# Low parts of the first phase's weights: VectorE in place of GpSimd

## The chip, the cores and the metric

The kernel runs on one core of one Trainium2 chip. The metric is the device time of one execution in microseconds (us). The core has five engines that each work through a queue of their own in order: TensorE (PE: matmuls; its weight loads have rows of their own, PEld), VectorE (DVE), ScalarE (ACT), GpSimd (POOL) and SyncE (SP, which issues most DMAs).

## The reference

One layer of a decoder trunk on 512 tokens, model width 2048, everything in fp32:

```python
mod = silu(c) @ w_ada + b_ada                       # 3 x 2048
shift, scale, gate = split(mod, 3)
u = rms_norm(x, norm_w) * (1 + scale) + shift       # 512 x 2048
proj = u @ w_in                                     # 512 x 23552
# three token mixers on slices of proj (differential attention,
# retention, dilated windows), each times silu of its gate slice
y_b = (mixer_b * silu(z_b)) @ P_b                   # three times
m = sum(sigmoid(g_b) * y_b)
out = rms_norm(x + gate * (m @ w_out), final_norm_w)
```

This case concerns the beginning: the modulation (scale and shift), u, and the first nine blocks of 128 columns of `w_in` that are multiplied with it, columns of the merge gate g_c.

## The kernel before

**Matmuls in two parts.** An fp32 operand a is split into a high part h = fp32r(a) and a low part l = a - h. A product is then three matmuls: high x high, high x low, low x high. ScalarE makes the high parts by a copy that rounds, and another engine makes the low parts by a subtraction of two SBUF tensors. A weight tile comes by DMA into `wr`; its high part is `wh`, its low part `wl`. For u they are `uh` and `ul`, 16 tiles each (one for each 128 rows of the model width). `wr`, `wh` and `wl` have three buffers each, so a load into `wr` waits until both parts of the tile three loads earlier have been made.

**The modulation by VectorE.** silu(c) @ w_ada is a product with one row, so it isn't done as a matmul: `mod_sum` multiplies tiles of `w_ada` (1 MB parts, `wa` and `wb`) by columns of silu(c) and adds them up in `acc`, one row block after another: 8 scalar_tensor_tensor instructions on 128x256 in a part, or 4 on 128x512. `mod_cols` then lets TensorE sum `acc` over the partitions (8 matmuls with a vector of `ones`), and VectorE adds bias and norm weight: the columns `s` (named `s1` in the code) for scale, `sh` for shift. There are 32 parts: 2 of 128 columns, 14 of 256 columns (two for each group of columns), 16 of 512 (four for each group).

**The stages around the change**, in order of time:

1. Start (to 32 us): x is loaded, normalized by VectorE and transposed by TensorE, and ScalarE copies the transposes to `xT`.
2. Phase 0 (32 to 127 us): 16 steps, one for each 128 rows k of the width. Step k multiplies seven column blocks of `w_in` with xT[k] times scale (`scaled(k)`: ScalarE makes `uh`, VectorE `ul`): 7 matmuls uh·wh, 7 ul·wh, 7 uh·wl, into seven PSUM banks. The shift isn't known yet, so its share is added later. In each step VectorE also sums one part of the modulation. Every second step `mod_cols` gives the scale of two further tiles.
3. Middle (127 to 154 us): the seven banks are copied out (`spill`), and two more column blocks are done as two halves of 8 x 3 matmuls each (`w_half`, 128x1024 weights). Four more parts of the modulation are summed.
4. Phase 1 (154 to 240 us): 16 steps as in phase 0 on the last seven column blocks of `w_in`, now with the whole u = xT·s + sh (`uf` by VectorE, then `uh`, `ul`); `uf` is also written to DRAM and has two buffers. The shift comes in four groups of four tiles.

After 240 us the rest of the layer follows, with weights whose low parts VectorE makes.

**Who makes the low parts.** In `split_first` (lines 267 to 270) GpSimd makes those of both phases' 32 steps. In the middle, `w_half` (line 172) is called with `low=nc.gpsimd` for the first of the two column blocks, and with VectorE for the second. All other calls of `w_half` use VectorE.

**What sets the order.** The order on each engine is not only that of the code: a scheduler places instructions by its own estimates, apart from places pinned by hand (`tc.issue_after` holds `scaled(k)` behind the ScalarE part of `split_first`, and the sum of a part behind `ul`). So a moved instruction also changes the order of its neighbours. Engines wait for one another by semaphores, and whatever stands behind a waiting instruction on its engine waits too.

Of the kernel before, what the change touches and what calls it, by code (L numbers as in the profile page):

```python
# [10 lines left out]
F32 = mybir.dt.float32  # L11
# [54 lines left out]
def hybrid_kernel(ctx, tc, x, c, w_in, w_pa, w_pb, w_pc, w_out, w_ada, b_ada, norm_w, lam,  # L66
                  da_w, ret_w, fin_w, k_ident, k_causal, k_band, k_tri4, k_sel, k_cos, k_sin,
                  k_decay, out):
    nc = tc.nc
# [18 lines left out]
    act, dve, pe, sync, pool = (Ordered(e) for e in (nc.scalar, nc.vector, nc.tensor, nc.sync, nc.gpsimd))  # L88
# [11 lines left out]
    def pj():  # L100
        return psum.tile([P, 512], F32, tag="pj", name="pj", bufs=2)

    def at():
        return psum.tile([P, 512], F32, tag="at", name="at", bufs=6)

    NF, NM = 7, 2
    w_in = w_in[0]
# [45 lines left out]
    def w_load(src, k0, c0):  # L153
        r, h, l = w_tiles([P, 8, P])
        sync.dma_start(out=r, in_=src[k0:k0 + 1024, c0:c0 + P].rearrange("(j p) c -> p j c", p=P))
        return r, h, l

    def w_half(src, k0, c0, rot=False, tiles=None, low=dve):

        if tiles is not None and len(tiles) == 2:  # L160
            return tiles
        r, h, l = tiles or w_load(src, k0, c0)
        if rot:
            for a in range(2):
                for e in range(2):
                    o = a * 64 + e * 32
                    rv = r[:, :, a * 64:a * 64 + 64].rearrange("p j (d e) -> p j e d", e=2)[:, :, e, :]
                    act.copy(h[:, :, o:o + 32], rv)
                    dve.tensor_sub(l[:, :, o:o + 32], rv, h[:, :, o:o + 32].bitcast(F32))
        else:  # L170
            act.copy(h, r)
            low.tensor_sub(l, r, h.bitcast(F32))  # L172
        return h, l

    def mm3(ps, ah, al, bh, bl, start, stop):
        pe.matmul(ps, lhsT=ah, rhs=bh, start=start, stop=False)
        pe.matmul(ps, lhsT=ah, rhs=bl, start=False, stop=False)
        pe.matmul(ps, lhsT=al, rhs=bh, start=False, stop=stop)
# [81 lines left out]
    def load_first(i):  # L260
        phase, k = steps[i]
        g0 = G_C + (0 if phase == 0 else NF + NM) * P
        r, h, l = w_tiles([P, NF, P])
        sync.dma_start(out=r, in_=w_in[k * P:(k + 1) * P, g0:g0 + NF * P].rearrange("p (b c) -> p b c", c=P))
        firsts[i] = (r, h, l)

    def split_first(i):
        r, h, l = firsts[i]
        halves[i] = act.copy(h, r).ins
        nc.gpsimd.tensor_sub(l, r, h.bitcast(F32))  # L270

    wb = [None]
    mod_load()
# [39 lines left out]
    def mod_cols(m):  # L313
        half, c0, cw = MODS[m]
        acc = accs.pop(m)
        pc = pj()
        nch = cw // P
        chains = min(2, 512 // cw)
        for ci in range(nch):
            for a in range(chains):  # L320
                pe.matmul(pc[:, ci:ci + 1], lhsT=acc[:, a, ci * P:(ci + 1) * P], rhs=ones[:, 0:1],
                                 start=a == 0, stop=a == chains - 1)
        mod_finish(m, pc)
# [14 lines left out]
    def mod_step(n=1):  # L338
        for _ in range(n):
            if to_sum:  # L340
                m, part = to_sum.pop(0)
                mod_sum(m, part)
                mod_load()
# [33 lines left out]
    def scaled(k):  # L377
        act.activation(out=uh[k], in_=xT[:, k, :], func=AF.Copy, scale=s1[:, k:k + 1])
        return dve.scalar_tensor_tensor(out=ul[k], in0=xT[:, k, :], scalar=s1[:, k:k + 1],
                                        in1=uh[k].bitcast(F32), op0=ALU.mult, op1=ALU.subtract).ins  # L380

    for k in range(KC):
        tp = tps[k] if k < 6 else at()
        for i in range(3 if k < 6 else 0, NT):
            x_tr(tp, i, k)
        act.copy(xT[:, k, :], tp)
        if k == 0:
            scaled(0)
            split_first(0)
            m, part = to_sum.pop(0)  # L390
            mod_sum(m, part)
            mod_cols(m)
        if k == 4:
            split_first(1)
# [4 lines left out]
    def spill(ps, db, on_act):  # L399
        raw = wbp.tile([P, S], F32, tag="raw", name="raw", bufs=2)  # L400
        if on_act:
            act.copy(raw, ps)
        else:
            dve.tensor_copy(raw, ps)
        nc.scalar.dma_start(out=graw_dram[db], in_=raw)

    mids = []
    group_of = {(1 - half) * KC + c0 // P: m for m, (half, c0, cw) in enumerate(MODS) if m > 1}
    for i, (phase, k) in enumerate(steps):
        if k == 0:  # L410
            ps = [at() for _ in range(6)] + [pj()]
        if i + 2 < KC or KC <= i < 2 * KC - 2:
            load_first(i + 2)
        elif phase == 0:
            mids.append(w_load(w_in, (i + 2 - KC) * 1024, G_C + NF * P))
        if phase == 0 and k > 0:
            with tc.issue_after(halves[i]):
                low_part = scaled(k)
        elif phase == 1:
            uf = wbp.tile([P, S], F32, tag="uf", name="uf", bufs=2)  # L420
            dve.tensor_scalar(out=uf, in0=xT[:, k, :], scalar1=s1[:, k:k + 1], scalar2=sh[:, k:k + 1],
                              op0=ALU.mult, op1=ALU.add)
            act.copy(uh[k], uf)
            dve.tensor_sub(ul[k], uf, uh[k].bitcast(F32))
            nc.scalar.dma_start(out=u_dram[k], in_=uf)
        if i in (KC, KC + 1):
            split_first(i)
        if i + 1 < 2 * KC and i + 1 not in (1, KC, KC + 1):
            split_first(i + 1)
        r, h, l = firsts.pop(i)  # L430
        for b in range(NF):
            pe.matmul(ps[b], lhsT=h[:, b, :], rhs=uh[k], start=k == 0, stop=False)
        if i + 1 < 2 * KC and i + 1 != KC and (i + 1) in group_of:
            mod_cols(group_of[i + 1])
        for b in range(NF):
            pe.matmul(ps[b], lhsT=h[:, b, :], rhs=ul[k], start=False, stop=False)
        for b in range(NF):
            pe.matmul(ps[b], lhsT=l[:, b, :], rhs=uh[k], start=False, stop=k == KC - 1)
        if phase == 0 and k > 0:
            with tc.issue_after(low_part):  # L440
                mod_step()
        else:
            mod_step(2 if i == 0 else 1)
        if k == KC - 1 and phase == 0:
            for b in range(NF):
                spill(ps[b], b, b % 2 == 0)
            if phase == 0:
                mids.append(w_load(w_in, 0, G_C + (NF + 1) * P))
                for b in range(NM):
                    pb = pj() if b == 0 else at()  # L450
                    for half in range(2):
                        h, l = w_half(w_in, 0, 0, tiles=mids.pop(0), low=nc.gpsimd if b == 0 else dve)
                        if b == 0 and half == 0:
                            mids.append(w_load(w_in, 1024, G_C + (NF + 1) * P))
                        elif (b, half) != (1, 1):
                            load_first(KC + b)
                        for j in range(8):
                            kk = half * 8 + j
                            if kk == 10 and b == 1:
                                mod_cols(group_of[KC])  # L460
                            mm3(pb, h[:, j, :], l[:, j, :], uh[kk], ul[kk], kk == 0, kk == KC - 1)
                        mod_step()
                    spill(pb, NF + b, True)
# [278 lines left out]
    def cut():  # L742
        if loads:
            tiles, rot = loads.pop(0)
            entry.append(w_half(None, 0, 0, rot, tiles))

    def step(*extra):

        feed()
        for f in extra:  # L750
            f()
        cut()
        due, late[:] = list(late), []
        for f in due:
            f()
        return entry.pop(0)
# [44 lines left out]
    for n in range(LAST):  # L801
        c0, cw = GROUPS[n]
# [337 lines left out]
    for hd in range(8):  # L1140
        h, prev = heads[hd], heads[hd - 1] if hd else None
# [545 lines left out]
    for n in range(LAST):  # L1687
# [3 lines left out]
        for t, k in enumerate(range(0, KC, nk)):  # L1691
# [17 lines left out]
            h, l = step()  # L1709
# [12 lines left out]
    c0, cw = GROUPS[LAST]  # L1722
    for f in waiting:
        f()
    for i in range(NT):
# [14 lines left out]
        h, cs = hx[i][3], slice(512 - cw, 512)  # L1740
# [31 lines left out]
```

## Time and profile before

| | |
|---|---|
| median of 3 runs | 2590.24 us (2589.38 to 2594.89) |
| profiled execution, own time | 2591.96 us |
| span of its trace | 2590.2 us |
| VectorE busy, whole span | 1924.0 us (74%) |
| GpSimd busy, whole span | 263.7 us (10%) |
| ScalarE busy, whole span | 1134.5 us (44%) |
| the 34 subtractions by GpSimd | 20.7 to 232.5 us |
| granted TensorE clock, mean of the span | 0.995 |

The views used: the **page** (busy time of each engine); the **windows** (busy time of each engine, instructions, granted clock and DMA share between two times); the **groups** (instructions of one line, engine, operation and shape: count | busy time, mean duration in ns | idle time before them and what ended it); the **waits** (who waited for whom: total, times, longest); the **timeline** (start, duration, engine, line, operation, count of merged instructions, and in brackets the idle time before with what ended it). Helpers record most operations, so nearly all rows have line L86; the tile names tell them apart. A tile name stands as out<-in: `wl<-wr,wh` is the subtraction in question. DVE durations in a row run from start to end of one instruction; consecutive ones overlap by some 0.07 us, so a merged row of n instructions is a little shorter than n durations.

### The profile page before, as it was taken

How to read it: one execution, taken by the hardware profiler on the slowest of the kernel's cores; microseconds unless marked ns; L12 is line 12 of the kernel's file. 1: busy time of each engine (PE TensorE's matmuls, PEld its weight loads, DVE VectorE, ACT ScalarE, POOL GpSimd, SP SyncE). 2: the span in 40 equal slices, each digit the busy share in tenths (PEclk: the TensorE clock that was granted, in tenths of full speed). 3: DMA queues.
4: the chain of work that ended last, by engine and by line, in shares of the span. 5: the costliest groups of instructions: out<-in, count | busy, mean ns of one | idle time of the engine just before them, and what ended most of it. 6: DMA issues, size and time to landing. Idle time of an engine off the chain costs nothing. (4 is left out here: it accounts for less than half of the span.)

```text
span 2590.2 us, 36747 instructions
## 1 busy us (share of the span) xinstructions
PE 2519.2 (97%) x14539; PEld 2222.9 (86%) x14539; DVE 1924.0 (74%) x2682; ACT 1134.5 (44%) x1476; POOL 263.7 (10%) x327
## 2 busy tenths in 40 slices
PE   6999999999999999999999999999999999999998
PEld 5777777999999999999888888888888888777888
DVE  7994788778877888778787777447877657776554
ACT  4233433443443333333345666346666436653223
POOL 3332000000000000000000000210000120003100
PEclk9999999999999999999999999999999999999999
DMA  9776755656666666666566555564343573348543
GB/s 345 262 277 214 268 209 207 221 194 221 236 233 212 223 214 238 233 217 225 206 211 199 147 148 147 179 188 130 91 122 114 165 239 97 107 126 286 196 132 114
DMA packets 363953, 504.83 MB, mean 195 GB/s; under 512 B 18850, under 2 KB 237748, under 8 KB 363396
## 3 DMA queue, kind: packets, MB, share of 16 engines
q1 hardware_dynamic: 329732, 401.89, 47.5%
q0 software_dynamic: 27136, 92.13, 10.4%
q10 hardware_dynamic: 6912, 8.46, 0.9%
q8 instruction: 114, 1.87, 0.3%
q14 instruction: 59, 0.48, 0.1%
HBM read 450.37 MB, written 52.04 MB: 194 GB/s over the span
## 5 line engine op out<-in xcount | busy, mean ns | idle before, releaser
L86 ACT CAST xh<-xr 128x2048 fp32r<-128x2048 f32 x196 | 374.4, 1910 | 589.1 <-PE at L86 471.0
L86 DVE TENSOR_TENSOR xl<-xr,xh 128x2048 fp32r<-128x2048 f32 x196 | 449.1, 2291 | 184.5 <-ACT xh L86 183.3
L86 PE MATMUL pj<-uh,wh 128*128 128x512 f32 x944 | 372.5, 395 | 0.0
L86 PE MATMUL pj<-uh,wl 128*128 128x512 f32 x944 | 369.4, 391 | 2.6 <-POOL wl L172 2.6
L86 PE MATMUL pj<-ul,wh 128*128 128x512 f32 x944 | 369.1, 391 | 0.0
L86 DVE TENSOR_TENSOR wl<-wr,wh 128x1024 fp32r<-128x1024 f32 (+2 forms) x241 | 238.2, 1007 | 174.8 <-ACT wh L86 173.8
L86 ACT CAST wh<-wr 128x1024 fp32r<-128x1024 f32 (+2 forms) x275 | 239.1, 889 | 285.5 <-PE at L86 136.2
L86 DVE TENSOR_TENSOR xr<-xr 128x512 f32<-128x512 f32 x448 | 309.2, 690 | 15.0 <-DMA xr<-in_w_in_dram 3.3
L86 PE MATMUL at<-fh,xl 128*128 128x256 f32 x864 | 245.0, 284 | 1.9 <-DVE xl L86 1.9
L86 PE MATMUL at<-fh,xh 128*128 128x256 f32 x864 | 244.5, 283 | 0.0
L86 PE MATMUL at<-fl,xh 128*128 128x256 f32 x864 | 244.5, 283 | 0.0
L86 PEld LDWEIGHTS pj<-uh,wl 128*128 128x128 f32 x944 | 178.0, 189 | 40.8 <-POOL wl L172 3.0
L86 PEld LDWEIGHTS pj<-uh,wh 128*128 128x128 f32 x944 | 178.4, 189 | 35.6
L86 PEld LDWEIGHTS pj<-ul,wh 128*128 128x128 f32 x944 | 178.2, 189 | 35.6
L86 PEld LDWEIGHTS at<-fh,xl 128*128 128x128 f32 x864 | 165.5, 192 | 2.3 <-DVE xl L86 2.3
L86 PEld LDWEIGHTS at<-fh,xh 128*128 128x128 f32 x864 | 165.5, 192 | 0.0
L86 PEld LDWEIGHTS at<-fl,xh 128*128 128x128 f32 x864 | 165.5, 192 | 0.0
L86 PE MATMUL at<-ul,xh 128*128 128x256 f32 x576 | 163.0, 283 | 0.0
L86 PE MATMUL at<-uh,xh 128*128 128x256 f32 x576 | 163.0, 283 | 0.0
L86 PE MATMUL at<-uh,xl 128*128 128x256 f32 x576 | 163.0, 283 | 0.0
L86 PE MATMUL at<-yh,wh 128*128 128x512 f32 x288 | 112.5, 390 | 2.1 <-ACT wh L86 2.1
L86 PE MATMUL at<-yh,wl 128*128 128x512 f32 x288 | 112.2, 390 | 0.5 <-DVE wl L86 0.5
(389 smaller groups left out, 5724.1 us busy)
## 6 DMA issues: line engine op xcount, KB each, us to landing
xr<-in_w_in_dram SPq DMA_DIRECT2D x224, 512.0 KB, 4.4
xr<-in_w_in_dram SPq DMA_DIRECT2D x84, 1024.0 KB, 4.8
wr<-in_w_in_dram SPq DMA_DIRECT2D x116, 512.0 KB, 4.0
wa<-in_w_ada_dram SPq DMA_DIRECT2D x20, 1024.0 KB, 8.5
wr<-in_w_out_dram SPq DMA_DIRECT2D x32, 512.0 KB, 3.9
wr<-in_w_in_dram SPq DMA_DIRECT2D x32, 448.0 KB, 8.5
wb<-in_w_ada_dram SPq DMA_DIRECT2D x12, 1024.0 KB
bw<-in_w_in_dram SPq DMA_DIRECT2D x24, 384.0 KB, 5.6
```

What stands on the lines that cost most here:

```text
L86: return lambda *a, **k: pin(f(*a, **k))
```

## The change

Both calls on GpSimd become calls on VectorE: the 32 subtractions of `split_first` (128x896, one for each step of both phases) and the two of the first column block in the middle (128x1024). The parameter `low` of `w_half`, no longer needed, goes.

```diff
-    def w_half(src, k0, c0, rot=False, tiles=None, low=dve):
+    def w_half(src, k0, c0, rot=False, tiles=None):
...
             act.copy(h, r)
-            low.tensor_sub(l, r, h.bitcast(F32))
+            dve.tensor_sub(l, r, h.bitcast(F32))
...
     def split_first(i):
         r, h, l = firsts[i]
         halves[i] = act.copy(h, r).ins
-        nc.gpsimd.tensor_sub(l, r, h.bitcast(F32))
+        dve.tensor_sub(l, r, h.bitcast(F32))
...
-                        h, l = w_half(w_in, 0, 0, tiles=mids.pop(0), low=nc.gpsimd if b == 0 else dve)
+                        h, l = w_half(w_in, 0, 0, tiles=mids.pop(0))
```

Data, tiles, buffers, DMAs and SyncE's order stay the same. GpSimd keeps nothing to do before its first DMA after phase 1, and the two instructions that configure it stand before its first tensor operation, now in the attention stage at 1407 us. The places where VectorE's order changes, in three pieces.

VectorE at the start, where the fourth tile of x is normalized. `ss` is the sum of squares, `rstd` the reciprocal root (ScalarE takes the root between these two), `x_157` the tile of x, `acc` the sum of a part, `ul_122` the first `ul`; + is new, - is gone:

```order
 L86 TENSOR_TENSOR ss<-ss 128x1
+L86 TENSOR_TENSOR wl<-wr,wh 128x896
 L86 RECIPROCAL rstd<-rstd 128x1
 L86 TENSOR_SCALAR x_157<-x_157,rstd 128x1024 x2
 L86 TENSOR_SCALAR acc<-wa,sc 128x128 x2
-L86 SCALAR_TENSOR_TENSOR acc<-wa,sc,acc 128x128 x2
+L86 SCALAR_TENSOR_TENSOR acc<-wa,sc,acc 128x128 x4
 L86 SCALAR_TENSOR_TENSOR ul_122<-xT,s_99,uh_106 128x512
```

The first step's `wl` now stands between the sum of squares and the reciprocal.

VectorE in phase 0, two steps, first before and then of the change. `ul_127` to `ul_129` are the `ul` of steps 5 to 7; `s_99` are the scale columns, which wait for the matmuls with `ones`:

```order
L86 SCALAR_TENSOR_TENSOR ul_127<-xT,s_99,uh_111 128x512
L86 TENSOR_SCALAR acc<-wb,sc 128x256 x2
L86 SCALAR_TENSOR_TENSOR acc<-wb,sc,acc 128x256 x3
L86 TENSOR_TENSOR s_99<-pj,cols 128x2
L86 SCALAR_TENSOR_TENSOR acc<-wb,sc,acc 128x256
L86 SCALAR_TENSOR_TENSOR s_99<-s_99,cols 128x2
L86 SCALAR_TENSOR_TENSOR acc<-wb,sc,acc 128x256 x2
L86 SCALAR_TENSOR_TENSOR ul_128<-xT,s_99,uh_112 128x512
L86 SCALAR_TENSOR_TENSOR acc<-wa,sc,acc 128x256 x8
L86 SCALAR_TENSOR_TENSOR ul_129<-xT,s_99,uh_113 128x512
```

```order
L86 SCALAR_TENSOR_TENSOR ul_127<-xT,s_99,uh_111 128x512
L86 TENSOR_SCALAR acc<-wb,sc 128x256 x2
L86 SCALAR_TENSOR_TENSOR acc<-wb,sc,acc 128x256
L86 TENSOR_TENSOR s_99<-pj,cols 128x2
L86 SCALAR_TENSOR_TENSOR acc<-wb,sc,acc 128x256
L86 SCALAR_TENSOR_TENSOR s_99<-s_99,cols 128x2
L86 SCALAR_TENSOR_TENSOR acc<-wb,sc,acc 128x256 x4
L86 TENSOR_TENSOR wl<-wr,wh 128x896
L86 SCALAR_TENSOR_TENSOR ul_128<-xT,s_99,uh_112 128x512
L86 SCALAR_TENSOR_TENSOR acc<-wa,sc,acc 128x256 x7
L86 TENSOR_TENSOR wl<-wr,wh 128x896
L86 SCALAR_TENSOR_TENSOR acc<-wa,sc,acc 128x256
```

In each step one `wl` now stands shortly before that step's `ul`, and the scale columns come two instructions earlier. The next row of the second list is `ul_129`.

VectorE in phase 1, from the `ul` of step 2 to the second group of shift columns; `sh` are these columns, `uf` is the new u:

```order
 L86 TENSOR_TENSOR ul_124<-uf,uh_108 128x512
+L86 TENSOR_TENSOR wl<-wr,wh 128x896
+L86 SCALAR_TENSOR_TENSOR acc<-wa,sc,acc 128x512
+L86 TENSOR_TENSOR ul_125<-uf,uh_109 128x512
 L86 SCALAR_TENSOR_TENSOR acc<-wa,sc,acc 128x512 x2
-L86 TENSOR_TENSOR ul_125<-uf,uh_109 128x512
+L86 TENSOR_TENSOR wl<-wr,wh 128x896
 L86 SCALAR_TENSOR_TENSOR acc<-wa,sc,acc 128x512 x5
+L86 TENSOR_TENSOR wl<-wr,wh 128x896
 L86 SCALAR_TENSOR_TENSOR acc<-wb,sc,acc 128x512 x4
 L86 TENSOR_TENSOR sh<-pj,cols 128x4
 L86 TENSOR_SCALAR acc<-wb,sc 128x512
```

Three subtractions now stand ahead of the shift columns, among the same sums. On TensorE the order of the steps stays; only the `ones` matmuls at the end of the start stage come four transposes earlier.

## The prediction

> **What bounds the kernel now.** First the page, then the windows of the three stages that the change touches (columns: time, length, busy time and instructions of PE, PEld, DVE, ACT, POOL, granted clock, DMA share, GB/s):
>
> ```profile
> PE 2519.2 (97%) x14539; PEld 2222.9 (86%) x14539; DVE 1924.0 (74%) x2682; ACT 1134.5 (44%) x1476; POOL 263.7 (10%) x327
> ...
> 31.00:126.60 95.60, 87.35 (x406) 70.03 (x405) 90.58 (x156) 27.00 (x38) 39.58 (x16) 1.00 0.88 300
> 126.60:153.60 27.00, 24.43 (x105) 19.96 (x104) 24.37 (x32) 8.23 (x11) 8.26 (x3) 0.94 0.80 285
> 153.60:239.70 86.10, 81.99 (x361) 67.44 (x361) 56.48 (x68) 25.50 (x34) 31.79 (x14) 0.96 0.63 222
> ```
>
> Over the whole span TensorE sets the time. Not so here: in phase 0 VectorE is busy for 90.6 of 95.6 us, more than TensorE's 87.3, and in the other two stages the granted clock is below 1. The waits of TensorE in the three stages, in this order, name who is late:
>
> ```profile
> PE at L86 <- DVE ul L86: 3.5, 2, 1.9
> PE pj L86 <- DVE acc L86: 2.8, 4, 0.7
> PE at L86 <- ACT uh L86: 2.0, 4, 0.9
> ...
> PE pj L86 <- POOL wl L172: 2.6, 1, 2.6
> ...
> PE at L86 <- ACT uh L86: 4.1, 2, 3.7
> ```
>
> `ul` and `acc` are VectorE's, and `uh` waits for scale or `uf`, VectorE's too. So the question is what VectorE's queue gains or loses. The timeline at the beginning of phase 0 shows what GpSimd does to it:
>
> ```profile
> 29.03 4.07 POOL L270 TENSOR_TENSOR wl<-wr,wh 128x896 fp32r<-128x896 f32 x1 [5.96 <-ACT wh L86]
> 31.36 2.02 DVE L86 SCALAR_TENSOR_TENSOR acc<-wa,sc,acc 128x256 f32<-128x256 f32 x1
> ...
> 38.61 3.95 POOL L270 TENSOR_TENSOR wl<-wr,wh 128x896 fp32r<-128x896 f32 x1 [5.51 <-ACT wh L86]
> 40.57 2.27 DVE L86 SCALAR_TENSOR_TENSOR acc<-wa,sc,acc 128x256 f32<-128x256 f32 x1
> ```
>
> One `acc` on 128x256, begun while GpSimd subtracts, takes over 2 us and ends 0.28 us after GpSimd's end (33.38 after 33.10, 42.84 after 42.56). It stands still until GpSimd is done.
>
> **What the change takes from VectorE's queue, and adds.** Groups: GpSimd's 32 subtractions; the sums in phase 0; the same shapes where no GpSimd subtraction runs; then the nearest relatives of the new instruction, `wl` on 128x1024 and `ul` on 128x512, both by VectorE from two SBUF tensors:
>
> ```profile
> L270 POOL TENSOR_TENSOR wl<-wr,wh 128x896 fp32r<-128x896 f32 x32 | 77.2, 2420 | 138.1 <-ACT wh L86 129.0 <-PE pj L86 9.1
> ...
> L86 DVE SCALAR_TENSOR_TENSOR acc<-wa,sc,acc 128x256 f32<-128x256 f32 x56 | 34.0, 667 | 0.0
> L86 DVE SCALAR_TENSOR_TENSOR acc<-wb,sc,acc 128x256 f32<-128x256 f32 x42 | 28.4, 741 | 0.0
> L86 DVE SCALAR_TENSOR_TENSOR acc<-wa,sc,acc 128x512 f32<-128x512 f32 x11 | 12.0, 1092 | 0.2
> ...
> L86 DVE SCALAR_TENSOR_TENSOR acc<-wa,sc,acc 128x256 f32<-128x256 f32 x11 | 4.4, 472 | 0.0
> ...
> L86 DVE SCALAR_TENSOR_TENSOR acc<-wa,sc,acc 128x512 f32<-128x512 f32 x2 | 1.5, 748 | 0.0
> ...
> L86 DVE TENSOR_TENSOR wl<-wr,wh 128x1024 fp32r<-128x1024 f32 x2 | 2.4, 1219 | 0.0
> ...
> L86 DVE TENSOR_TENSOR ul<-uf,uh 128x512 fp32r<-128x512 f32 x2 | 1.4, 678 | 0.0
> ```
>
> Lost in phase 0 by standing still: 56 x (667 - 472) + 42 x (741 - 472) + 11 x (1092 - 748) ns = 10.9 + 11.3 + 3.8 = **26.0 us**. Added: 512 columns more cost 1219 - 678 = 541 ns, so 128x896 takes 1219 - 135 = 1084 ns, some 1.02 us of the queue since neighbours overlap (an estimate from these two rows). Phase 0 gets 14 of them and one of 128x1024: **15.5 us**. So VectorE gives away 26.0 and takes 15.5, and its busy time there falls from 90.6 to about 80.1 us. The gain is the standing still, not GpSimd's own time.
>
> One page of the Trainium skill speaks against the change: Perfetto Trace Analysis, section Optimizing Scalar/DVE Operations, says that when VectorE is saturated, handing work to ScalarE or even GpSimd can pay; it adds that the two share a port of SBUF, so that moving work between them might not help. The first half would keep GpSimd's share where it is; the rows above go with the second half, 26.0 us lost against 15.5 us of work.
>
> **Start, -1.3 us.**
>
> ```profile
> 19.70 0.93 ACT L86 CAST wh<-wr 128x896 fp32r<-128x896 f32 x1
> ...
> 21.05 2.03 DVE L86 TENSOR_TENSOR ss<-ss 128x1 f32<-128x1 f32 x1
> 23.12 0.29 ACT L86 ACTIVATE rstd<-ss,eps 128x1 f32<-128x1 f32 x1 [2.49 <-DVE ss L86]
> ```
>
> An addition of one column, `ss`, takes 2.03 us, because it too stands behind GpSimd's first subtraction. Without that it ends at about 21.15. The new `wl`, whose `wh` is ready at 20.63, fills VectorE to 22.2, while ScalarE takes the root; then the normalization goes on, at 22.3 in place of some 23.6 (23.12 + 0.29 and the reciprocal). The fourth tile's transposes and the copies behind them follow. Bounds: 0 to 1.9.
>
> **Phase 0, -9.5 us.** The first matmul, and one pair of steps on TensorE:
>
> ```profile
> 32.15 0.48 PE L86 MATMUL at<-uh,wh 128*128 128x512 f32 x1
> ...
> 98.03 1.13 PE L86 MATMUL pj<-ones,acc 128*128 128x1 f32 x8 [0.75 <-DVE acc L86]
> 99.03 1.63 PE L86 MATMUL at<-ul,wh 128*128 128x512 f32 x6
> ...
> 106.27 1.52 PE L86 MATMUL at<-uh,wl 128*128 128x512 f32 x6
> ...
> 107.86 1.52 PE L86 MATMUL at<-uh,wh 128*128 128x512 f32 x6
> ...
> 110.32 1.13 PE L86 MATMUL pj<-ones,acc 128*128 128x1 f32 x8 [0.72 <-DVE acc L86]
> ```
>
> The pair lasts 12.3 us. Seven matmuls need 1.59 us (106.27 to 107.86), a step of 21 thus 4.77, the `ones` 1.0: without waits the pair would last 10.5. Sixteen steps and seven groups of `ones` make 83.3 us; phase 0 now lasts 94.5 (32.15 to 126.6, where the middle's first matmul stands). So at most 11.2 us can go. VectorE alone would allow 10.5 (90.6 to 80.1, with the same 5 us of idle time). Both limits come out nearly alike, so I look at the order in a pair. After the scale columns VectorE does four sums (1.6 us), `wl` (1.0) and `ul` (0.7), so `ul` is there 3.5 us after the `ones`; TensorE wants it 4.8 us after (three blocks of seven). Both steps of the pair come out with 1 to 2 us to spare, and the sums are complete well ahead of the next `ones`. I leave out 1 us for steps 2 to 4, where the weights still arrive at the pace of the DMA and `wl` with `ul` (1.7 us) follows `wh` while TensorE has only 1.6 us to do. Bounds: -11.2, and -5 if half of the waits stay.
>
> **Middle, -2.8 us.**
>
> ```profile
> 135.24 0.79 PE L86 MATMUL pj<-uh,wl 128*128 128x512 f32 x1 [2.57 <-POOL wl L172]
> 135.83 0.63 PE L86 MATMUL pj<-uh,wh 128*128 128x512 f32 x1
> ...
> 138.69 0.39 PE L86 MATMUL pj<-ul,wh 128*128 128x512 f32 x1
> ```
>
> TensorE waits 2.57 us for GpSimd's second 128x1024, then its first nine matmuls take 3.45 us in place of 9 x 0.227 = 2.05: the clock was taken back, 1.4 us more. Now this `wl` stands in VectorE's queue, behind 11 sums on 128x512 (0.67 us each: 0.75 less the overlap), a scaling, two copies and the other `wl` since the last `ul`: 11.4 us. TensorE has 40 matmuls, 9.1 us, until it wants it. If VectorE comes in 1.2 us ahead, the wait shrinks to about 1.1 us and the slow stretch goes. Bounds: -4.0, and -0.3 with the clock still lost.
>
> **Phase 1, -5.0 us.**
>
> ```profile
> 149.65 0.16 DVE L86 TENSOR_TENSOR sh<-pj,cols 128x4 f32<-128x4 f32 x1 [2.35 <-PE pj L86]
> ...
> 159.55 5.13 DVE L86 SCALAR_TENSOR_TENSOR acc<-wa,sc,acc 128x512 f32<-128x512 f32 x2
> ...
> 165.21 5.69 DVE L86 SCALAR_TENSOR_TENSOR acc<-wa,sc,acc 128x512 f32<-128x512 f32 x5
> ...
> 170.93 4.85 DVE L86 SCALAR_TENSOR_TENSOR acc<-wb,sc,acc 128x512 f32<-128x512 f32 x4
> 175.70 0.15 DVE L86 TENSOR_TENSOR sh<-pj,cols 128x4 f32<-128x4 f32 x1
> ...
> 177.41 2.93 PE L86 MATMUL at<-uh,wh 128*128 128x512 f32 x6 [3.66 <-ACT uh L86]
> ...
> 183.26 1.55 PE L86 MATMUL at<-uh,wl 128*128 128x512 f32 x6
> ```
>
> From the first shift columns to the second VectorE takes 26.05 us. Eleven sums in it last 15.7 us and would last 7.6 (11 x 0.67, and 0.08 for each of three stretches): 8.1 us of standing still. Three `wl` cost 3.1. So the second columns come after 21 us, `uf`, `uh` 1.7 us later, at 23; if the wait of `uf` for its buffer grows, at 24.7. TensorE, which starts phase 1 at 153.6, 4.0 us after the first columns, wants `uh` after 4.0 + 4 x 4.77 + 1.0 = 24.1 us. A wait of 0 to 0.6 replaces 3.66, and the slow stretch behind it goes (177.41 to 183.26 is 5.85 us for two sevens that need 3.18: 2.67). Together -5.7 to -6.3. Against that, at step 8 two `wl` stand ahead of the third shift columns: +1.0. Bounds: -7, and -1.5 if the clock is lost again.
>
> **The rest, 0.** No DMA is added and SyncE's order stays; a `wr` buffer comes free when VectorE is done in place of GpSimd, later by a few us in phase 0, while loads run two steps ahead. GpSimd has nothing queued behind the 34 instructions before its first DMA after phase 1. TensorE is the bound afterwards, so what is gained stays.
>
> **Sum.** 1.3 + 9.5 + 2.8 + 5.0 = 18.6 us off the profiled execution's 2591.96 (its span 2590.2 and 1.8 around it): 2573.4. The median of the runs is 1.7 us below that execution, so I say 2572.
>
> **Rivals.**
>
> - *VectorE's queue holds it up.* `wl` waits for ScalarE's `wh` and so for DMA; `ul`, sums and columns wait behind it, where GpSimd waited alone before. For: 0.88 DMA share in phase 0, and `wl` directly ahead of `ul`. Against: 1 to 2 us to spare in every pair. Price: with half of phase 0's gain, no gain in the middle, 1.5 in phase 1 and 0.7 at the start the sum is 5 + 0.3 + 1.5 + 0.7 = 7.5 us: 2583. Chance 0.14.
> - *No change.* The waits go but TensorE gets others of the same size, from `uh` by ScalarE above all: 2590. Against: ScalarE is busy for 27 of 95.6 us. Chance 0.07.
> - *Slower: VectorE is overloaded.* If the long sums have another cause than GpSimd, they stay long, and a queue with 5 us of idle time gets 15.5 us more in phase 0: +10.5 there, and 2 in the middle, 2603. It decides from the point where less than 10.5 of the 26.0 us go. This is what the Trainium skill's advice on a saturated VectorE would mean here. Against: each long `acc` ends with GpSimd's subtraction. Chance 0.05.
> - *The change doesn't do what it says*: GpSimd's time is hidden and gives nothing. It is contained in "no change".
>
> **How the numbers follow.** Forecast 0.74, the held-up queue 0.14, no change 0.07, slower 0.05. The bounds of the terms add to -24 and -7; the range from 2565 to 2584 takes in the forecast's bounds and the first rival. A measurement of this kernel tells about 0.2%, 5 us, from no change: forecast and first rival are faster (0.87 with a little off the first), no change 0.08, slower 0.05.
>
> **What would show it.** In the changed profile no `acc` on 128x256 takes over 0.6 us, `ss` takes under 0.2, phase 0 lasts 83 to 87 us, VectorE is busy for about 80 us in it, `wl` on 128x896 takes 1.08 us; the granted clock in the middle and in phase 1 is 0.98 or more. The prediction is wrong if `acc` stays long, or if TensorE waits for `wl` or `ul` in most steps.

## The result and the profile after

The changed kernel takes **2575.32 us** (median of 4 runs, 2571.79 to 2576.98), the kernel before 2591.72 beside it (4 runs, 2589.38 to 2594.89). The ratio is 0.9933 [0.9921, 0.9945]: 0.67% faster. The profiled execution took 2571.79 us, its span 2570.0. Before, it was 2591.96.

The windows of the same three stages in the changed kernel (columns as before: time, length, busy time and instructions of PE, PEld, DVE, ACT, POOL, granted clock, DMA share, GB/s), its waits of TensorE up to 225 us, and the groups of VectorE in phase 0:

```profile
30.80:114.10 83.30, 82.88 (x395) 69.38 (x394) 77.10 (x168) 25.75 (x35) 0.00 (x0) 1.00 0.96 328
114.10:142.30 28.20, 24.57 (x105) 20.01 (x104) 21.25 (x30) 8.04 (x11) 0.00 (x0) 0.94 0.91 324
142.30:221.80 79.50, 79.49 (x362) 65.64 (x361) 56.83 (x86) 25.87 (x35) 0.00 (x0) 1.00 0.68 240
```

```profile
PE pj L86 <- DVE wl L86: 3.6, 1, 3.6
PE at L86 <- DVE ul L86: 0.4, 1, 0.4
```

```profile
L86 DVE SCALAR_TENSOR_TENSOR acc<-wa,sc,acc 128x256 f32<-128x256 f32 x55 | 23.1, 477 | 0.0
L86 DVE SCALAR_TENSOR_TENSOR acc<-wb,sc,acc 128x256 f32<-128x256 f32 x42 | 17.6, 480 | 0.0
L86 DVE TENSOR_TENSOR wl<-wr,wh 128x896 fp32r<-128x896 f32 x14 | 15.2, 1086 | 0.0
...
L86 DVE SCALAR_TENSOR_TENSOR acc<-wa,sc,acc 128x512 f32<-128x512 f32 x11 | 8.2, 746 | 0.1
```

In phase 0 TensorE is busy for 82.9 of 83.3 us: it is the bound there now. VectorE has taken over 15 subtractions and is nevertheless busy for 77.1 us in place of 90.6. A sum on 128x256 takes 477 to 480 ns on average in place of 667 to 741. The means of before hide two kinds: 12 of the 98 sums took 2.02 to 2.36 us, each under another subtraction of GpSimd's, and the others some 0.47; now none takes over 0.485. In phase 1 no wait of TensorE is left. In the middle one wait is left, and it is longer than before: 3.62 us, with the granted clock at 0.94.

The stages as the table has them run from the first matmul of one to the first of the next, so a wait ahead of a stage's first matmul counts for the stage before it. The last column holds the rest, to the last matmul. All times are of the profiled executions, in us.

| kernel | start | phase 0 | middle | phase 1 | middle + phase 1 | rest |
|---|---|---|---|---|---|---|
| before | 32.2 | 94.5 | 27.0 | 86.1 | 113.2 | 2341.6 |
| changed | 30.8 | 83.3 | 28.2 | 79.4 | 107.6 | 2339.1 |
| e1_early | 30.8 | 83.3 | 27.3 | 80.0 | 107.2 | 2344.6 |
| e2_mid_gpsimd | 31.8 | 83.4 | 28.9 | 79.2 | 108.1 | 2342.9 |
| e3_twice | 32.8 | 99.4 | 29.5 | 93.9 | 123.4 | 2339.2 |
| e4_phase0_only | 30.5 | 83.4 | 30.1 | 85.6 | 115.7 | 2342.9 |
| e5_ahead | 30.3 | 83.3 | 29.2 | 81.9 | 111.1 | 2343.2 |
| e6_ahead_three | 31.1 | 83.3 | 23.9 | 85.9 | 109.8 | 2340.7 |
| e7_phase1_only | 31.3 | 94.5 | 25.6 | 79.3 | 104.9 | 2340.5 |
| e8_twice_copy | 31.3 | 85.3 | 28.8 | 83.0 | 111.8 | 2339.4 |
| e9_shared_early | 30.8 | 83.3 | 24.9 | 79.0 | 104.0 | 2342.7 |
| e10_shared_ahead | 30.7 | 83.3 | 25.6 | 79.1 | 104.7 | 2339.9 |
| e11_shared | 31.1 | 83.3 | 29.6 | 80.6 | 110.2 | 2340.0 |

(The three stages multiply sixteen blocks of 128 columns: seven, two and seven.) Phase 0 repeats within 0.1 us wherever its work is the same. The rest, whose code is the same in all of them, differs by up to 5.5 us. So a difference of 2 or 3 us between two totals tells little here, and the stages tell more.

From before to after: start -1.3, phase 0 -11.2, middle **+1.1**, phase 1 -6.7, together -18.0 us (from 239.77 to 221.75). Why the middle went the wrong way is seen in the timeline of the changed kernel there (start, duration, engine and so on, idle time before in brackets):

```profile
113.42 0.68 DVE L86 COPY raw<-at 128x512 f32<-128x512 f32 x1
113.58 0.88 ACTq L405 DMA_DIRECT2D graw<-raw  x2
...
114.50 1.05 ACT L86 CAST wh<-wr 128x1024 fp32r<-128x1024 f32 x1 [0.95 <-DVE raw L86]
...
120.63 0.58 ACT L86 COPY raw<-at 128x512 f32<-128x512 f32 x1 [5.07 <-DMA graw<-raw]
...
121.27 0.69 DVE L86 COPY raw<-at 128x512 f32<-128x512 f32 x1 [3.86 <-DMA graw<-raw]
121.87 0.74 DVE L86 SCALAR_TENSOR_TENSOR acc<-wa,sc,acc 128x512 f32<-128x512 f32 x1
122.53 1.22 DVE L86 TENSOR_TENSOR wl<-wr,wh 128x1024 fp32r<-128x1024 f32 x1
...
123.81 0.60 PE L86 MATMUL pj<-uh,wl 128*128 128x512 f32 x1 [3.62 <-DVE wl L86]
124.20 0.63 PE L86 MATMUL pj<-uh,wh 128*128 128x512 f32 x1
```

The second `wl` has its input at 115.55 (114.50 + 1.05) and starts at 122.53. VectorE isn't overloaded: it stands still for 3.86 us, because the copy of a bank into `raw` waits for one of two `raw` buffers, and both are still being written to `graw` in DRAM. Those writes were issued at 113.58. Without the 3.86 us `wl` would end at 119.9, and TensorE wanted it at 120.19.

### The profile page after: what moved, and what is told of

Its sections match the earlier page's. It is cut to its first block, busy times and chain, and to the rows that moved or that the text cites. A ratio compares the mean times of both kernels' runs of the same rounds, so it can differ in the third digit from the quotient of the medians.

```text
span 2570.0 us, 36726 instructions
## 1 busy us (share of the span) xinstructions
PE 2516.9 (98%) x14539; PEld 2224.0 (87%) x14539; DVE 1907.0 (74%) x2716; ACT 1134.4 (44%) x1476; POOL 179.9 (7%) x293
## 5 line engine op out<-in xcount | busy, mean ns | idle before, releaser
L86 DVE TENSOR_TENSOR wl<-wr,wh 128x1024 fp32r<-128x1024 f32 (+2 forms) x275 | 275.4, 1018 | 186.2 <-ACT wh L86 181.4
```

Source lines behind the costliest of these rows:

```text
L86: return lambda *a, **k: pin(f(*a, **k))
```

## The experiments

Two theories stood after the result. **One: the lock.** VectorE's sums stand still while GpSimd works on SBUF, as if it had locked them out, and the gain comes from the end of that, not from GpSimd's own lateness. The rival: GpSimd's `wl` was late, and VectorE delivers it sooner. (In the kernel before no wait of TensorE in the two phases is for a `wl` of GpSimd's; only the one of 2.57 us in the middle is.) **Two: the head of the queue.** What is lost in the middle is VectorE's waiting for DMA writes; the rivals are too much work on VectorE, and the pace of the loads. The edits below are made to the changed kernel where nothing else is said.

**GpSimd's work put back beside VectorE's.** Both kernels compute everything; a GpSimd instruction on the same tiles is added, whose result nobody reads.

```diff
         dve.tensor_sub(l, r, h.bitcast(F32))
+        spare = wp.tile([P, 6, P], F32R, tag="spare", name="spare")
+        nc.gpsimd.tensor_sub(spare, r[:, 0:6, :], h[:, 0:6, :].bitcast(F32))
```

> The change, and in both phases GpSimd also subtracts 128x768 of the same two tiles into a spare tile that nobody reads. Theory (VectorE stands still while GpSimd subtracts): the sums of 128x256 take over 2 us again, VectorE has the subtractions and the standing still: phase 0 lasts 100 to 110 us in place of 83, the time is 2595 to 2612 us, above the kernel before. Rival (the gain came from wl being made in 1.1 in place of 2.4 us): wl is still made by VectorE, the sums stay short, 2574 to 2577 us.

Measured: 2609.32 us (2605.44 to 2614.9), 1.0068 [1.0054, 1.0082] of before. Timeline of e3_twice in phase 0, then a group over its span:

```profile
59.10 2.09 POOL L272 TENSOR_TENSOR spare<-wr,wh 128x768 fp32r<-128x768 f32 x1 [2.08 <-ACT wh L86]
59.42 2.32 DVE L86 SCALAR_TENSOR_TENSOR ul<-xT,s,uh 128x512 fp32r<-128x512 f32 x1
...
61.79 1.65 PE L86 MATMUL at<-ul,wh 128*128 128x512 f32 x6 [1.04 <-DVE ul L86]
```

```profile
L272 POOL TENSOR_TENSOR spare<-wr,wh 128x768 fp32r<-128x768 f32 x32 | 77.3, 2415 | 168.7 <-ACT wh L86 152.8 <-issue 14.8 <-POOL spare L272 0.5
```

`ul` ends 0.55 us after GpSimd (61.74 after 61.19), and TensorE waits for it. Nobody needs what GpSimd makes, yet its 77.3 us, as many as before the change, cost 16.1 us in phase 0 and 34 us in all. In phase 0 TensorE waits 6.8 us for `ul` and 2.8 us for `acc`, VectorE's both, and never for a weight; a load waits for GpSimd to release its buffer only once, for 1.7 us. GpSimd needn't be late to cost time: the lock holds, its rival falls.

The same with a copy, which reads one tensor:

```diff
+        spare = wp.tile([P, 6, P], F32, tag="spare", name="spare")
+        nc.gpsimd.tensor_copy(spare, h[:, 0:6, :].bitcast(F32))
```

> The change, and in both phases GpSimd also copies 128x768 of the high part, one input, into a spare tile that nobody reads. Theory a (VectorE stands still whenever GpSimd works on SBUF): the sums of 128x256 that meet a copy take as long as the copy, 1 us or more, phase 0 lasts 88 to 100 us, 2582 to 2600 us. Theory b (only GpSimd instructions with two inputs stop VectorE): the sums stay at 0.47 us, phase 0 at 83.3 us, 2574 to 2577 us.

Measured: 2582.1 us (2578.68 to 2584.85), 0.9968 [0.9956, 0.998]; phase 0 2.0 us longer than in the changed kernel. In the timeline of e8_twice_copy a copy by GpSimd holds VectorE too:

```profile
63.77 1.08 DVE L86 TENSOR_TENSOR wl<-wr,wh 128x896 fp32r<-128x896 f32 x1
63.98 1.56 POOL L272 COPY spare<-wh 128x768 f32<-128x768 f32 x1 [3.72 <-ACT wh L86]
64.77 1.31 DVE L86 SCALAR_TENSOR_TENSOR ul<-xT,s,uh 128x512 fp32r<-128x512 f32 x1
```

`ul` ends 0.54 us after the copy and takes 1.31 us; where no copy meets it, it takes 0.74. Eight of the 98 sums on 128x256 took over 0.6 us, up to 1.06, which speaks against theory b; but phase 0 lasted 85.3 us, less than theory a's 88 to 100. The copies last 1.24 us on average in place of 2.42, so each holds less.

**Each stage by itself.** Subtractions back on GpSimd outside phase 0, then outside phase 1, then in the middle alone (in all three the middle has GpSimd for its first block, as before). These three are edits to one line of the kernel before:

```diff
-        nc.gpsimd.tensor_sub(l, r, h.bitcast(F32))
+        (dve if i < KC else nc.gpsimd).tensor_sub(l, r, h.bitcast(F32))
```

> Only phase 0's 16 subtractions on VectorE, the middle's two and phase 1's 16 on GpSimd. Theory: start and phase 0 as in the changed kernel (1 and 11 us), the middle with a wait under 1 us, phase 1 as before with its wait of 3.7 us: 2577 to 2580 us. Rival (each part's gain only counts with the others, since TensorE meets VectorE later): under 6 us below the kernel before, 2586 us or more.

Measured: 2581.42 us (2579.49 to 2583.67), 0.9959 [0.9945, 0.9972], a little over the expectation, since the middle lost 3 us against before: TensorE waits 2.9 us there, not under 1, for a `wl` by VectorE, which waited 2.0 us for a write into `graw`. With `i >= KC` in place of `i < KC`:

> Only phase 1's 16 subtractions on VectorE, phase 0's and the middle's on GpSimd. Theory (each stage by itself: VectorE's standing still in that stage): start and phase 0 as before (94.5 us), phase 1 79 to 80 us in place of 86.1, the time 2584 to 2586 us. Rival (phase 1 gains only because phase 0 hands VectorE over in time): phase 1 stays above 83 us, 2589 us or more.

Measured: 2583.94 us (2581.35 to 2587.22), 0.9973 [0.9963, 0.9983], at the lower end of what was expected. The table shows the parts to be separate: phase 0 is 83.4 or 94.5 us, phase 1 79.3 or 85.6, each by who makes its own low parts.

With both phases on VectorE (`dve.tensor_sub` in that line) and only the middle's two on GpSimd:

> The change in both phases, but the two subtractions of the middle back on GpSimd. Theory (VectorE's queue): GpSimd has nothing else to do, starts when wh is there and is done in 3.4 us, about when TensorE wants it: a wait under 1 us, 2570 to 2572 us, with two short standstills of VectorE that nobody waits for. Rival (GpSimd's 3.4 us were themselves the cause of the wait of 2.57 us before): a wait of 2 to 3 us and the slow clock come back, 2574 to 2576 us.

Measured: 2575.7 us (2572.04 to 2577.49), 0.9936 [0.9923, 0.9948], middle 28.9 us. The time is the rival's, but not for its reason: TensorE has no wait for a `wl` of GpSimd's. GpSimd's 3.63 us hold one sum for 2.29 us, and VectorE's third `wl` comes late all the same. From the timeline of e2_mid_gpsimd:

```profile
116.17 3.63 POOL L172 TENSOR_TENSOR wl<-wr,wh 128x1024 fp32r<-128x1024 f32 x1 [6.61 <-ACT wh L86]
...
129.13 0.69 DVE L86 COPY raw<-at 128x512 f32<-128x512 f32 x1 [1.97 <-DMA graw<-raw]
129.73 2.35 DVE L86 TENSOR_TENSOR wl<-wr,wh 128x1024 fp32r<-128x1024 f32 x2
...
131.01 0.50 PE L86 MATMUL at<-uh,wl 128*128 128x512 f32 x1 [2.89 <-DVE wl L86]
```

So the middle isn't lost because VectorE took over its first two: with GpSimd it is no better.

**The order in the middle.** The first block's two splits are written ahead of the copies:

```diff
+            first_two = [w_half(w_in, 0, 0, tiles=mids.pop(0)) for _ in range(2)]
             for b in range(NF):
                 spill(ps[b], b, b % 2 == 0)
...
-                        h, l = w_half(w_in, 0, 0, tiles=mids.pop(0))
+                        h, l = first_two[half] if b == 0 else w_half(w_in, 0, 0, tiles=mids.pop(0))
```

> The change, with the first two subtractions of the middle written ahead of the copies of the seven banks; VectorE's order then has the second one just ahead of its second copy. Theory (VectorE's queue: the copy waits for a DMA write that frees its buffer, and wl stands behind it): TensorE's wait of 3.62 us in the middle and the slow clock after it (about 1.5 us) go, 5 us below the changed kernel: about 2570 us. Rival (the subtraction waits for its own input, by ScalarE or the DMA): the wait stays, 2575 us.

Measured: 2573.47 us (2572.75 to 2576.86), 0.9932 [0.9919, 0.9944], in place of the 2570 expected, the middle only 0.9 us shorter. The wait for the second `wl` is gone as foreseen, but the timeline of e1_early shows it handed on to the third `wl`:

```profile
125.75 0.69 DVE L86 COPY raw<-at 128x512 f32<-128x512 f32 x1 [1.75 <-DMA graw<-raw]
...
127.02 1.22 DVE L86 TENSOR_TENSOR wl<-wr,wh 128x1024 fp32r<-128x1024 f32 x1
...
128.29 0.66 PE L86 MATMUL at<-uh,wl 128*128 128x512 f32 x1 [2.69 <-DVE wl L86]
```

Then all four splits between the copies: two ahead of the first copy, the third ahead of the third, the fourth ahead of the fifth; and the same with three `raw` buffers.

```diff
-            for b in range(NF):
+            ready = [w_half(w_in, 0, 0, tiles=mids.pop(0)) for _ in range(2)]
+            third = w_load(w_in, 0, G_C + (NF + 1) * P)
+            for b in range(2):
+                spill(ps[b], b, b % 2 == 0)
+            ready.append(w_half(w_in, 0, 0, tiles=third))
...
-        raw = wbp.tile([P, S], F32, tag="raw", name="raw", bufs=2)
+        raw = wbp.tile([P, S], F32, tag="raw", name="raw", bufs=3)
```

> The change, with all four splits of the middle written between the copies of the banks: two ahead of the first copy, one ahead of the third, one ahead of the fifth; two copy buffers as before. Theory (in the middle the splits stand in VectorE's and ScalarE's queues behind copies that wait for DMA writes, so that moving one split ahead only hands the wait to the next): the wait of 3.6 us and that of 2.7 us that took its place both shrink, the middle lasts 24 to 25 us in place of 28.2, the time is 2570 to 2572 us. Rival (the weights of the second block arrive late): the middle stays at 27 to 28 us, 2574 us.

> As the kernel with the splits written between the copies, and three copy buffers in place of two. Theory (copies waiting for DMA writes): a copy waits for the write three copies earlier, so less stands still behind it: the middle lasts 23 to 24 us (22.7 without any wait), 2569 to 2571 us. Rival (weights arrive late): no difference from two buffers.

Both expectations missed the total: 2578.77 us (2575.74 to 2579.43), 0.995 [0.9938, 0.9962], and with three buffers 2575.92 (2573.93 to 2578.74), 0.9943 [0.993, 0.9955]. In the first, TensorE waits 4.37 us for `uh` at phase 1's beginning (the table counts it in the middle, 29.2 us). There ScalarE's queue is held: a copy into `raw` waits 4.90 us for a write, and VectorE 3.31 us for the `wh` behind it. In the second the middle is 23.9 us, as expected, but phase 1 gives the gain back. The timeline of e6_ahead_three there:

```profile
143.75 0.55 DVE L86 TENSOR_SCALAR uf<-xT,s,sh 128x512 f32<-128x512 f32 x1 [2.68 <-DMA ud<-uf]
...
146.38 0.55 DVE L86 TENSOR_SCALAR uf<-xT,s,sh 128x512 f32<-128x512 f32 x1 [1.42 <-DMA ud<-uf]
...
160.65 0.15 DVE L86 TENSOR_TENSOR sh<-pj,cols 128x4 f32<-128x4 f32 x1
...
162.37 2.93 PE L86 MATMUL at<-uh,wh 128*128 128x512 f32 x6 [3.48 <-ACT uh L86]
```

VectorE again stands at the head of its queue for a DMA write, now for the two buffers of `uf`: 4.1 us. The columns `sh` come that much later, `uf` and `uh` behind them, and TensorE waits 3.48 us.

**The buffers.** `raw` and `uf` have the same shape and follow one another, so they can share five buffers in the room of two each and one more:

```diff
-        raw = wbp.tile([P, S], F32, tag="raw", name="raw", bufs=2)
+        raw = wbp.tile([P, S], F32, tag="raw", name="raw", bufs=5)
...
-            uf = wbp.tile([P, S], F32, tag="uf", name="uf", bufs=2)
+            uf = wbp.tile([P, S], F32, tag="raw", name="uf", bufs=5)
```

With the order of e1_early, with that of e6_ahead_three, and with the changed kernel's own:

> As e1_early, but raw and uf share five buffers in place of two each, so that a copy of the middle waits for a write to DRAM three copies later than before, and no uf waits for one (2.84 us in e1_early, 1.5 us in the changed kernel). Theory (what is won in the middle is given back because VectorE stands at the head of its queue for a DMA write, first in raw, then in uf): no wait of VectorE for graw or ud over 0.5 us, no wait of TensorE for wl in the middle, its clock kept; middle 24 to 25 us (27.25 in e1_early, 28.18 in the changed kernel), phase 1 78.5 to 81, so the two together 103 to 106 in place of 107.2, total 2569 to 2572. Rival (the weights of phase 1 and the parts of the modulation arrive at the pace of the DMA, and TensorE waits for whatever needs them last): the waits for buffers go but the two stages together stay at 107 to 108, total as e1_early, 2573.

> As e6_ahead_three, with the five shared buffers. Theory: the 4.1 us that VectorE waits for the writes of uf in e6_ahead_three go, the second group of shift columns comes some 4 us earlier, and with it uh; the wait of 3.48 us in phase 1 and the slow matmuls behind it go. The scheduler now puts five sums ahead of the first uf (3.4 us), so the start of phase 1 waits up to 2 to 3 us for uh. Middle 24 (23.94 before, up to 27 with the wait at its end), phase 1 79 to 81, the two together 103 to 107 in place of 109.8, total 2569 to 2573. Rival (DMA pace): the two together stay at 109 to 110, total 2576.

> The changed kernel with the five shared buffers and its own order of the code. Theory: the copies of the middle no longer wait for a write (5.07 us and 3.86 us in the changed kernel), but the scheduler now puts the low parts of the middle behind more sums and the first shift columns, so wl may still be late, behind work instead of behind a wait: middle 25 to 28, phase 1 79 to 82, total 2571 to 2576. Rival (DMA pace): middle 28, phase 1 80, total 2575, with the wait for wl still over 3 us though VectorE is never idle in front of it.

The first two came out as the theory has it: 2571.76 us (2568.4 to 2573.41), 0.9925 [0.9912, 0.9939], and 2572.96 (2569.42 to 2573.95), 0.9929 [0.9916, 0.9941]. VectorE has no wait for a write of `uf` and none over 1.2 us for one of `raw`; in the two stages no wait of TensorE for `wl` and no lost clock is left; middle and phase 1 together last 104.0 and 104.7 us in place of 107.6. So the loads' pace isn't what held the two stages at 107.6. What remains is at phase 1's beginning, in the timeline of e9_shared_early:

```profile
133.83 0.15 DVE L86 TENSOR_TENSOR sh<-pj,cols 128x4 f32<-128x4 f32 x1
...
134.96 2.98 DVE L86 SCALAR_TENSOR_TENSOR acc<-wa,sc,acc 128x512 f32<-128x512 f32 x4
137.86 1.45 DVE L86 TENSOR_SCALAR uf<-xT,s,sh 128x512 f32<-128x512 f32 x3
...
139.10 1.67 PE L86 MATMUL at<-uh,wh 128*128 128x512 f32 x6 [2.12 <-ACT uh L86]
```

The scheduler puts 4 us of sums between the columns and the first `uf`. The third kernel, buffers alone, missed its expectation: 2576.47 us (2574.39 to 2580.72), 0.9949 [0.9936, 0.9961], with the middle at 29.6. The scheduler reordered VectorE's queue, the first `uf` came behind more sums (2.64 us of waiting), and the clock was lost. Buffers helped only together with the order.

Against the changed kernel e9_shared_early wins 3.6 us in the stages (190.9 to 187.3 from phase 0 to phase 1). The totals, 2575.32 and 2571.76, point the same way, but their ranges overlap, and the kernel before, run beside each, took 2591.72 and 2589.69: by that the gains are 16.4 and 17.9 us (16.7 for e10_shared_ahead), too near to tell apart.

## Why the prediction was right, and where not

**Start, -1.3 predicted, -1.3 measured.** The addition `ss` takes 0.15 us in place of 2.03, and the reciprocal starts at 21.65. But 0.44 us of the 1.3 are an earlier arrival of the first small load, which the change doesn't touch; that the two numbers agree so closely is in part luck.

**Phase 0, -9.5 predicted, -11.2 measured**, the lower bound. The mechanism was right: the longest of the 112 `acc` instructions on 128x256 takes 0.485 us, below the 0.6 named, and a `wl` takes 1086 ns (predicted 1084). VectorE's busy time fell to 77.1 us, not 80. The sum counted only `acc` sums as held, but a scaling `acc<-wb,sc` was held too, which is 1.9 of these 3 us, as this row of before shows (two instructions, 2.48 us in place of 0.61 for a pair that isn't held); the rest wasn't traced:

```profile
50.60 2.48 DVE L86 TENSOR_SCALAR acc<-wb,sc 128x256 f32<-128x256 f32 x2
50.63 2.30 POOL L270 TENSOR_TENSOR wl<-wr,wh 128x896 fp32r<-128x896 f32 x1 [0.74 <-ACT wh L86]
```

And the 1 us reserved for steps 2 to 4 was too much: one wait of 0.42 us is all that is left, and phase 0 takes the 83.3 us that the prediction worked out for 16 steps and seven groups of `ones`. The rival with VectorE overloaded fell with this, and e3_twice shows what it would have needed: GpSimd still at work.

What the Trainium skill says on this, page SBUF — State Buffer, section SBUF: two separate sides, is that the port pair which VectorE and GpSimd share is an exclusive lock for a whole instruction, and that an operation of VectorE with two SBUF inputs meets it only against a GpSimd operation that reads SBUF. The runs agree: the 12 sums on 128x256 that stood still beside GpSimd's subtractions do so no more without them, and a GpSimd copy, which reads one tensor, makes eight sums slow again (over 0.6 us).

**Middle, -2.8 predicted, +1.1 measured: the step that failed.** The prediction said of the second `wl`: "behind 11 sums on 128x512 ..., a scaling, two copies and the other `wl` since the last `ul`: 11.4 us". It counted the copies by their duration, 0.6 us each. It didn't ask whether they wait. One of them waited 3.86 us for a DMA write. GpSimd's queue had nothing of the kind ahead of its `wl`; VectorE's had. That is the prediction's first rival, a queue that holds it up, in one place and with another releaser: it named ScalarE's `wh`, and it was a write to DRAM. As a result the granted clock, predicted at 0.98 or more, is 0.94 there. The working of the queue was otherwise right: the same instructions stand there, and from the end of the last `ul` (108.65) to the end of this `wl` (123.75) they take 15.1 us, without the 3.86 us 11.2. `wl` would then have come 0.3 us ahead of TensorE.

**Phase 1, -5.0 predicted, -6.7 measured.** The wait of 3.66 us and the slow stretch behind it are gone, as foreseen (5.7 to 6.3 us), and so is a second wait, of 0.46 us. The 1.0 us taken off for step 8 wasn't needed: no wait is left there.

**The rest and the sum.** Predicted -18.6 us from the profiled execution, and the four terms came to -18.0. That is close because the middle, 3.9 us worse than predicted, was offset by the two phases, 1.7 us better each. Execution against execution it is -20.2; the 2.2 beyond the terms lie in the rest and are within what it varies by. By the medians the change is -16.4 us, where the prediction has -18.2 (2590.24 to 2572): the profiled execution was the fastest of the four.

## What to carry to other kernels

Before moving work off an engine to relieve it, look in the trace for instructions of it that last several times their normal duration and end together with one of the other engine: GpSimd's help cost VectorE more than doing the work itself, and even work that nobody waits for cost 34 us. When an instruction moves into another queue, list what stands ahead of it there, and for each not only its duration but what it waits for; a copy into a buffer that a DMA still empties holds all behind it. If a stage's gain shows up as a new wait in the next stage, it can be, as here, the same kind of wait on the next pair of buffers, and order and buffers may have to be changed together.

## What the runs showed of the hardware

**What a short wait costs depends on where it falls.** Two nearly equal waits on GpSimd's second `wl`, of 2.57 us in the kernel before and 2.58 us in e7_phase1_only, ended differently. Timeline of e7_phase1_only:

```profile
134.48 0.50 PE L86 MATMUL pj<-uh,wl 128*128 128x512 f32 x1 [2.58 <-POOL wl L172]
134.82 0.39 PE L86 MATMUL pj<-uh,wh 128*128 128x512 f32 x1
135.04 0.40 PE L86 MATMUL pj<-ul,wh 128*128 128x512 f32 x1
```

Here the matmuls soon start 0.22 us apart again, at full clock. In the kernel before they were slow for 3.45 us (135.24 to 138.69), and in the changed kernel after 3.62 us of waiting for 3.4 us. The traces show why. All changes of the granted clock in a trace lie on one grid of 3.41 us: in the kernel before at 135.13, 138.54, 176.09 and 182.91 us, that is 1, 11 and 2 steps apart, and likewise over the whole span of each of the 13 runs, with an offset of its own. Two cells of this grid from the kernel before, then two from e7_phase1_only (columns as in the windows above):

```profile
131.72:135.13 3.41, 0.95 (x5) 0.45 (x3) 3.41 (x4) 1.09 (x2) 3.41 (x1) 1.00 0.40 151
135.13:138.54 3.41, 3.30 (x8) 2.63 (x9) 3.30 (x5) 1.38 (x2) 0.05 (x1) 0.50 0.83 252
130.19:133.60 3.41, 1.72 (x8) 1.10 (x6) 3.41 (x6) 1.04 (x3) 3.10 (x1) 1.00 0.29 109
133.60:137.02 3.42, 2.54 (x11) 2.10 (x12) 3.31 (x4) 2.16 (x3) 0.83 (x1) 1.00 0.83 255
```

The wait of before lies almost whole in one cell, where TensorE is busy for only 0.95 us, and the next cell has half the clock. In e7_phase1_only the wait falls into two cells, and neither costs the clock. In the 13 traces all 56 cells at full clock with over 2 us of idle time of TensorE were followed by one at half the clock; of the 76 with 1.4 to 2 us it was 26, and of all the others two. The Trainium skill, page TensorE: Matmul & The Clock Gate, section What's actually happening, puts the gate's window at 3413 ns and calls it free-running. The length of the slow stretches and the grid agree with that. But waits shorter than a window can cost the clock, while the page speaks of a whole idle window; here the runs decide. One of those last two cells is in e11_shared: it (120.95 to 124.36) holds only two waits, of 0.48 and 0.22 us, and cost the clock too. The timeline of TensorE there:

```profile
120.95 1.02 PE L86 MATMUL pj<-ones,acc 128*128 128x1 f32 x8 [0.93 <-DVE acc L86]
122.46 0.50 PE L86 MATMUL pj<-uh,wh 128*128 128x512 f32 x1 [0.48 <-ACT wh L86]
...
123.41 0.51 PE L86 MATMUL at<-uh,wh 128*128 128x512 f32 x1 [0.22 <-ACT wh L86]
...
124.76 0.63 PE L86 MATMUL pj<-ul,wh 128*128 128x512 f32 x1
```

From 124.36 to 127.75 the matmuls there start 0.43 us apart. Another 1.02 us of that cell went to the eight `ones` matmuls, which are one column wide; whether these count as idle was not tried. So a wait's price has two values, itself or some 1.6 us more for each slow cell (eight matmuls 0.43 us apart in place of 0.227), and one execution can't tell which a kernel mostly gets, since the grid's offset differs.

**More of VectorE's instructions are held than the sums**: an addition of one column (2.03 us, in the prediction's rows), and the scaling of one tensor by a column (by 1.9 us, the 2.48 less 0.61 above; in phase 1 of before also a `uf` at 203.07, 1.44 us in place of 0.53). What decides for the scaling was not tried. Not held was `s<-pj,cols`, with one input in PSUM, at 31.28: it took its usual 0.16 us while GpSimd subtracted. GpSimd waits as well: the subtraction at 29.03, of 4.07 us, began while six sums on 128x128 and two scalings of VectorE ran at their usual lengths until 31.13, 1.97 us before it ended.
